# Stick-breaking attention weights: sigmoids and a running product in place of logarithms, sums and an exponential

## The chip, the core and the metric

The kernel runs on one core of a Trainium2 chip. The metric is device time in microseconds (us), lower is better. The median of three runs before the change is 1969.86 us (1965.07 to 1970.98).

The engines have short names here: PE multiplies matrices (PEld is its loading of weights), DVE is VectorE, ACT is ScalarE, POOL is GpSimd, and SP issues the transfers.

## The reference

Two blocks run one after the other on 512 tokens of 1024 features: the first has sparse attention and retention, the second a feed-forward part, a mixer, attention over a memory, and another feed-forward part. The change lies in the mixer, in its stick-breaking attention of 16 heads of 64 features. Cut to that:

```python
def stick_breaking_attention(q, k, v):
    """A[t,s] = beta_ts * prod_{s<j<t}(1-beta_tj), s<t."""
    scale = 1.0 / math.sqrt(d_)
    for i in range(s_ // SB_BLOCK):                       # blocks of 128 queries
        z = jnp.einsum('bhtd,bhsd->bhts', qb, kb) * scale  # keys up to the block's end
        causal = s_idx[None, :] < t_idx[:, None]
        log_1mb = jnp.where(causal, jax.nn.log_sigmoid(-z), 0.0)
        suffix = lax.cumsum(log_1mb, axis=3, reverse=True) - log_1mb
        log_a = jnp.where(causal, jax.nn.log_sigmoid(z) + suffix, -jnp.inf)
        outs.append(jnp.einsum('bhts,bhsd->bhtd', jnp.exp(log_a), vb))
```

A query's weight for a key is sigmoid(z) of that key times the product of sigmoid(-z) over the keys between the two.

## The kernel before

All matrix products with weights are made of three products of split numbers: the upper bits of one operand (`whi`, `a_hi`, written by ACT at L82) and the rest (`wlo`, `a_lo`, written by DVE at L83). `proj_T` (L158) gives results with the features on the partitions, `proj_X` (L203) with the tokens there. The weights come in pieces of 512 KB through three buffers `raw`.

The stick-breaking part runs over eight pairs of heads (`p`). For each pair, `proj_T` makes the queries and the keys in PSUM banks mm0 and mm1; they are split (L82, L83, L85, L86), and transfers issued by SP (L972, L975) lay them out as `Q` and `K`, two buffers each. The four query tiles of 128 then come in three groups: tiles 0 and 1 together (128 + 256 = 384 columns of scores), tile 2 (384) and tile 3 (512). A group of one head is called a unit here: 8 x 3 x 2 = 48 units. A unit goes through these steps:

- L987: the scores in one PSUM bank `sb`, two products for each query tile. Even heads use the pool `sp` (two banks), odd heads banks mm2 and mm3; the last pair uses `sp` for both.
- L991 to L993 on ACT: Abs, Exp and Ln, so that with L994 on DVE `l` becomes the softplus of the score.
- L999 on DVE: the running sum of `l` from the last key backwards. The constant `keep` holds the sum at 1e30 up to the query's own key, restarts it there and lets it run from there on. One scan for each query tile, 64 in all.
- L1000 on DVE: score minus sum, which reads the scores' bank once more; L1001 on ACT: its exponential, the weights, in one of four buffers `cs`.
- L1006 on PE: transposes into the one PSUM bank `tp`; L1008 copies them to SBUF as `aT`, on ACT for the even head and on DVE for the odd one.
- L1015 on PE: products with the values, summed in the bank `ob`; L1017 copies it out at the end of the pair, and L1022 and L1023 add up squares for the norm that follows.

That norm (L1029 to L1038) takes a logarithm and an exponential on ACT (L1034, L1035). It scales the attention's output, which is split into `oat_hi` and `oat_lo`, the second half of the features that the out-projection (L203) takes in; the first half is the state space part, transposed at L230.

The order of the instructions on each engine isn't that of the program text. A planner lays out all engines' queues when the program is built, by its own estimate of durations, and earlier text has precedence. So the next pair's projections (L158) lie between the current pair's steps on PE, and behind the last pair come the transposes L230 and the out-projection. On the chip each queue runs in the order that the plan gave it.

Of the kernel before, what the change touches and what calls it, by code (L numbers as in the profile page):

```python
# [7 lines left out]
F32 = mybir.dt.float32  # L8
F32R = mybir.dt.float32r
AF = mybir.ActivationFunctionType  # L10
ALU = mybir.AluOpType
AX = mybir.AxisListType
PSUM = bass.MemoryType.PSUM
# [9 lines left out]
# column offsets in the constant arrays  # L23
# [8 lines left out]
def block_kernel(ctx, tc, A, out, upto=99):  # L32
# [28 lines left out]
    def bcast(src, n, tile_):  # L61
        """A vector of n values on every partition."""
        nc.sync.dma_start(tile_, bass.AP(tensor=src.tensor, offset=src.offset, ap=[[0, 128], [1, n]]))
        return tile_
# [6 lines left out]
    def rpow(v, mul, eps, n=1):  # L71
        """(v * mul + eps) ** -0.5 of a [128, n] tile."""
# [6 lines left out]
    def split(hi, lo, src, scale=None):  # L79
        """hi + lo = src (times scale): the upper bits and the rest."""  # L80
# [23 lines left out]
    clock, pend = [0.0], []  # L104

    def tick(n):
        """Counts a product of n columns, and puts in what is due."""
# [13 lines left out]
    def bank(of=(0, 1, 2, 3)):  # L121
        """The next of some PSUM banks for products."""
# [6 lines left out]
    def act_get(pair, k0=0):  # L129
        """Tokens t0..t1 of feature tile k, of activations kept as [128, token tile, k, 128]."""  # L130
# [6 lines left out]
    def proj_T(src, c0, ncols, get, consume, K=8, nt=NT, splits=None, of=(0, 1, 2, 3)):  # L137
        """Features on partitions: for each 128 columns, consume(tile index, [128, tokens] in PSUM)."""
# [25 lines left out]
    def lead_T(groups, get, slots, splits=((0, 2), (2, 4))):  # L164
        """A phase's first two groups of 256 columns (source, column, consume), over the first tokens before the others."""
# [22 lines left out]
    def proj_X(src, c0, w, get, consume, K=8, nt=NT, tail=1, kp=2, korder=None, between=None, slots=()):  # L188
        """Tokens on partitions: for each token tile, consume(t, [128, w] in PSUM)."""
# [31 lines left out]
    def transpose_split(src, n, dst_pair, t, scale=None, k0=0, of=None):  # L221
        """n 128-column tiles of a token tile [128, ., 512], transposed, to hi and lo at [:, t, k0:k0+n]."""
# [28 lines left out]
    def post_pre(src, K, get, g_post, half_scale, g_pre, fg, last=False, dst=None, korder=None, slots=(), tail=1, delay=DELAY):  # L251
        """x += norm(activations @ src) [* 0.5]; returns the next phase's normalised activations."""
# [39 lines left out]
    # =====================================================================  # L292
    # first block
    # =====================================================================
    def first_block():
# [32 lines left out]
        # --- compressed, selected and window keys, values and gates; queries times -1/8  # L328
# [8 lines left out]
        def rope(xv, nh, t):  # L337
            """xv [128, nh, >=16]: rotates its first 16 columns in place."""
# [8 lines left out]
        def doubled(xv, nh):  # L347
            """Each head's 64 columns twice, transposed: [64 | 64 again, head, token] in PSUM."""
# [51 lines left out]
        # gates: 1 / (1 + exp(-x))  # L400
# [6 lines left out]
        # --- compressed blocks: the keys' hidden layer on partitions 0 to 63, the values' on 64 to 127  # L407
# [64 lines left out]
        # --- attention, three branches: scores have the sign turned, so that the least is the greatest; outputs as [2 heads x 64, token]  # L472
# [6 lines left out]
        def attention(qi):  # L479
# [4 lines left out]
            # compressed  # L484
# [27 lines left out]
            # selected, window  # L512
# [49 lines left out]
        def ev_zn(j, bank):  # L562
            """2 silu(z) = (tanh(z / 2) + 1) z"""
# [9 lines left out]
        # --- retention  # L573
# [81 lines left out]
        # --- gates of the two branches, in features layout: 2 sigmoid(m) = tanh(m / 2) + 1  # L655
# [10 lines left out]
        # --- outputs of the branches, merged  # L666
# [30 lines left out]
    # =====================================================================  # L697
    # gated feed-forward
    # =====================================================================
# [38 lines left out]
    # =====================================================================  # L738
# [486 lines left out]
```

## Time and profile before

| | |
|---|---|
| median of three runs | 1969.86 us |
| lowest and highest run | 1965.07 and 1970.98 us |
| span of the profiled execution, first to last instruction | 1963.4 us |
| busy in the span: PE, PEld, DVE, ACT | 1917.5, 1557.6, 1027.1, 773.2 us |
| the stick-breaking loop, scores of the first pair to the sum of squares of the last | 1160 to 1343 us |

The profiled execution's own time around its span isn't given; the runs above are other executions. Times in the rows below are counted from the span's start. A row of a group gives how many instructions there are, their busy time together, the mean of one in ns, and the engine's idle time just before them with what ended it. A PE instruction's end is modelled, so two that follow each other overlap as they are drawn: the time from one start to the next says what one costs. A wait put down to "issue" is one for which the profile shows no releaser. PEclk is the clock that PE was granted, as a share of 2.4 GHz.

### The profile page before, as it was taken

The page shows a single profiled execution, that of the slowest core. Times are in us where ns is not written, and L with a number is a line of the kernel's source. Part 1 is how long each engine was busy: PE and PEld are TensorE (multiplying, and loading weights), DVE is VectorE, ACT ScalarE, POOL GpSimd, SP SyncE. Part 2 cuts the span into 40 slices and gives each one's busy share as a digit, 9 for nine tenths or more (in the row PEclk, how much of TensorE's full clock was granted, in tenths as well). Part 3 has the DMA queues.
Part 4 walks back from the last instruction along what each step waited for, and adds up shares of the span by engine and source line. Part 5 has one row for each costly group of instructions (what it writes and reads, how often), then busy time and mean ns, then how long its engine had stood idle before and what let it go on. Part 6 is the DMA issues. An engine that isn't in the chain of part 4 may idle for free.

```text
span 1963.4 us, 24345 instructions
## 1 busy us (share of the span) xinstructions
PE 1917.5 (98%) x9676; PEld 1557.6 (79%) x9676; DVE 1027.1 (52%) x1751; ACT 773.2 (39%) x1332; POOL 39.2 (2%) x66
## 2 busy tenths in 40 slices
PE   7999999999999999999999999999999999999998
PEld 6777788788878888888877777667788888888887
DVE  5578743824563333323668658887464553333223
ACT  4345533223343232223545457775353432323221
POOL 0000000100000000000000000000000000000000
PEclk9999999999999999999999999999999999999999
DMA  7411033232332333324231355542262322333322
GB/s 243 129 44 33 23 97 97 83 100 86 97 101 93 97 96 97 97 97 129 83 87 43 86 135 129 129 118 68 84 192 87 97 65 86 97 97 97 97 97 86
DMA packets 153706, 191.38 MB, mean 97 GB/s; under 512 B 9748, under 2 KB 111480, under 8 KB 153464
## 3 DMA queue, kind: packets, MB, share of 16 engines
q1 hardware_dynamic: 153592, 189.82, 32.4%
q8 instruction: 76, 1.25, 0.3%
q14 instruction: 38, 0.31, 0.0%
HBM read 175.11 MB, written 2.10 MB: 90 GB/s over the span
## 4 chain that ended last, share of the span: by engine, by line
PE 84%; DVE 7%; ACT 2%; POOL 1%; issue 1%; DMA 1%; SPq 0%; POOLq 0%; DVEq 0%; ACTq 0%
PE mm L158 41%; PE mm L203 28%; PE mm L181 3%; PE ob L1015 1%; PE ob L555 1%; POOL rp_r L76 1%; DVE x_sb L273 1%; DVE cs L999 1%; PE tp L1006 1%; DVE h L245 1%; PE ob L896 1%; PE s L530 1%; PE s L1100 1%; DVE fg L266 1%; PE mm L547 1%
## 5 line engine op out<-in xcount | busy, mean ns | idle before, releaser
L83 DVE TENSOR_TENSOR wlo<-raw,whi 128x1024 fp32r<-128x1024 f32 (+1 forms) x276 | 335.8, 1217 | 652.4 <-ACT whi L82 647.1
L82 ACT ACTIVATE whi<-raw 128x1024 fp32r<-128x1024 f32 (+1 forms) x276 | 291.0, 1055 | 665.4 <-PE mm L203 282.1
L158 PE MATMUL mm<-a_hi,wlo 128*128 128x512 f32 x1120 | 439.9, 393 | 2.0 <-DVE wlo L83 1.9
L158 PE MATMUL mm<-a_hi,whi 128*128 128x512 f32 x1120 | 440.7, 393 | 0.0
L158 PE MATMUL mm<-a_lo,whi 128*128 128x512 f32 x1120 | 440.3, 393 | 0.0
L158 PEld LDWEIGHTS mm<-a_hi,wlo 128*128 128x128 f32 x1120 | 210.4, 188 | 45.5 <-DVE wlo L83 2.7
L158 PEld LDWEIGHTS mm<-a_hi,whi 128*128 128x128 f32 x1120 | 210.4, 188 | 43.5 <-issue 1.4
L158 PEld LDWEIGHTS mm<-a_lo,whi 128*128 128x128 f32 x1120 | 210.5, 188 | 43.2 <-issue 2.6
L203 PE MATMUL mm<-whi,a_hi 128*128 128x512 f32 (+1 forms) x400 | 157.2, 393 | 0.8 <-ACT whi L82 0.8
L203 PE MATMUL mm<-whi,a_lo 128*128 128x512 f32 (+1 forms) x400 | 157.2, 393 | 0.0
L203 PE MATMUL mm<-wlo,a_hi 128*128 128x512 f32 (+1 forms) x400 | 155.6, 391 | 0.0
L203 PE MATMUL mm<-whi,hid_hi 128*128 128x512 f32 x288 | 112.0, 389 | 0.0
L203 PE MATMUL mm<-whi,hid_lo 128*128 128x512 f32 x288 | 112.0, 389 | 0.0
L203 PE MATMUL mm<-wlo,hid_hi 128*128 128x512 f32 x288 | 112.0, 389 | 0.0
L203 PEld LDWEIGHTS mm<-whi,a_hi 128*128 128x128 f32 x400 | 75.7, 189 | 18.1 <-issue 2.5
L203 PEld LDWEIGHTS mm<-whi,a_lo 128*128 128x128 f32 x400 | 75.8, 189 | 15.9 <-issue 2.5
L203 PEld LDWEIGHTS mm<-wlo,a_hi 128*128 128x128 f32 x400 | 75.1, 188 | 15.0 <-issue 1.9
L76 POOL TENSOR_TENSOR rp_r<-rp_a,half 128x1 f32<-128x1 f32 (+1 forms) x58 | 37.1, 640 | 1894.0 <-DVE rp_a L74 1568.5
L203 PEld LDWEIGHTS mm<-whi,hid_hi 128*128 128x128 f32 x288 | 54.1, 188 | 11.2
L203 PEld LDWEIGHTS mm<-whi,hid_lo 128*128 128x128 f32 x288 | 54.1, 188 | 11.2
L203 PEld LDWEIGHTS mm<-wlo,hid_hi 128*128 128x128 f32 x288 | 54.1, 188 | 11.2
L82 ACT ACTIVATE hid_hi<-sg 128x512 fp32r<-128x512 f32 x44 | 27.4, 623 | 61.9 <-DVE sg L720 61.9
(442 smaller groups left out, 2961.4 us busy)
## 6 DMA issues: line engine op xcount, KB each, us to landing
raw<-in_w_in_dram SPq DMA_DIRECT2D x96, 512.0 KB, 3.7
raw<-in_ffn_w_gu_dram SPq DMA_DIRECT2D x88, 512.0 KB, 3.6
raw<-in_ffn_w_down_dram SPq DMA_DIRECT2D x44, 512.0 KB, 3.7
raw<-in_w_out_dram SPq DMA_DIRECT2D x24, 512.0 KB, 3.7
raw<-in_xa_wkv_dram SPq DMA_DIRECT2D x16, 512.0 KB, 3.7
raw<-in_w_ret_o_dram SPq DMA_DIRECT2D x8, 512.0 KB, 3.4
K<-kh SPq DMA_DIRECT2D x32, 128.0 KB, 2.4
K<-kl SPq DMA_DIRECT2D x32, 128.0 KB, 2.3
```

What stands on the lines that cost most here:

```text
L76: POOL.tensor_tensor(r[:, :n], a[:, :n], half[:, :n], op=ALU.pow)
L82: ACT.activation(hi, src, AF.Copy)
L83: V.tensor_tensor(lo, src, hi.bitcast(F32), op=ALU.subtract)
L158: PE.matmul(o, a, b, start=(kc + k == 0 and n == 0 and si == 0), stop=(kc + k == K - 1 and n == 2), skip_group_check=True)
L181: PE.matmul(banks[g][j][:, t0 * 128:t1 * 128], a, b, start=(kc + k + n + si == 0), stop=(kc == 1 and k == 3 and n == 2), skip_group_check= ...
L203: PE.matmul(banks[t][:, :w], a, b, start=(kk == 0 and n == 0), stop=(kk == K - 1 and n == 2))
L245: V.scalar_tensor_tensor(h, src, r, g, op0=ALU.mult, op1=ALU.mult)
L266: V.tensor_tensor(fgt, bank, gpost[:, hf * 512:(hf + 1) * 512], op=ALU.mult)
L273: V.scalar_tensor_tensor(xs, fg[:, t if q == 0 else NT + t % 2], r, xs, op0=ALU.mult, op1=ALU.add)
L530: PE.matmul(sbs[e], qS[:, h, qsl], kk[:, br, g, :W], start=(n == 0 and (e == 0 or nk > 2)), stop=(n == 1), skip_group_check=True)
L547: PE.transpose(tp[:, o + j], p[:, e, j * 128:(j + 1) * 128], ident)
L555: PE.matmul(ob[64 * e:64 * e + 64, a], vv[:, j, br, g * 64:(g + 1) * 64], pT[:, e, j], start=False, stop=(br == 1 and j == nk - 1), skip_g ...
```

## The change

The logarithms go. The mask is added to the scores on PE: `far` holds the identity and a triangle of -2^99 at and above the diagonal of a query tile's own 128 keys, and one more product per query tile adds it to the bank. ACT then makes sigmoid(-z) (`l`, two buffers) and sigmoid(z) (`be`, three buffers). DVE's scan forms the running product of `l` from the last key backwards, as multiply and then maximum with `own1`, whose triangle holds the product at one down to the query's own key; it lies in tiles `E2` and `E1`, which are one column longer for each query tile. `be` times that product, shifted by one key, is the weight, in one instruction per unit, or two for the first group. The table of sigmoids is preloaded in place of that of exponential and logarithm, and `keep` isn't loaded any more. The rest of the diff is comments that are left out.

```diff
-        tc.keep_in_program_order(ACT.preload_act_table_set("natural_log_exp_and_others"))
-        keep = a1.tile([128, 512], F32, name="keep")
-        nc.sync.dma_start(keep, A["c_k"])
+        tc.keep_in_program_order(ACT.preload_act_table_set("sigmoid_and_others"))
+        own1 = a1.tile([128, 512], F32, name="own1")
+        V.memset(own1[:, 0:384], 0.0)
+        V.tensor_copy(own1[:, 384:512], tri)
+        E2 = [a1.tile([128, 386], F32, name=f"E2{e}") for e in range(2)]
+        E1 = [a1.tile([128, 513], F32, name=f"E1{n}") for n in range(3)]
+        for e in E2:
+            V.memset(e[:, 128:129], 1.0)
+            V.memset(e[:, 385:386], 1.0)
+        for e in E1:
+            V.memset(e[:, 512:513], 1.0)
+        n1 = [0]
+        far = a1.tile([128, 2, 128], F32R, name="far")
+        ACT.copy(far[:, 0], ident)
+        ACT.activation(far[:, 1], tri, AF.Copy, scale=-(2.0 ** 99))
...
                             first = False
-                    l = a2.tile([128, 512], F32, name="l", bufs=4)
-                    ACT.activation(l[:, :T], sb[:, :T], AF.Abs)
-                    ACT.activation(l[:, :T], l[:, :T], AF.Exp, scale=-1.0)
-                    ACT.activation(l[:, :T], l[:, :T], AF.Ln, bias=1.0)
-                    V.scalar_tensor_tensor(l[:, :T], sb[:, :T], 0.0, l[:, :T], op0=ALU.max, op1=ALU.add)
-                    cs = a2.tile([128, 512], F32, name="cs", bufs=4)
-                    for i, off in segs:
-                        W = (i + 1) * 128
-                        rev = slice(off + W - 1, (off - 1) if off else None, -1)
-                        V.tensor_tensor_scan(cs[:, rev], keep[:, 511:(511 - W) if W < 512 else None:-1], l[:, rev], 1e30, op0=ALU.mult, op1=ALU.add)
-                    V.tensor_tensor(cs[:, :T], sb[:, :T], cs[:, :T], op=ALU.subtract)
-                    ACT.activation(cs[:, :T], cs[:, :T], AF.Exp)
-                    css.append(cs)
+                        PE.matmul(sb[:, off + i * 128:off + W], far[:, 0], far[:, 1], start=False, stop=True, skip_group_check=True)
+                    l = a2.tile([128, 512], F32, name="l")
+                    ACT.activation(l[:, :T], sb[:, :T], AF.Sigmoid, scale=-1.0)
+                    be = a2.tile([128, 512], F32, name="be", bufs=3)
+                    ACT.activation(be[:, :T], sb[:, :T], AF.Sigmoid)
+                    if len(segs) == 2:
+                        E, at = E2[e], ((0, 0), (128, 129))
+                    else:
+                        E, at = E1[n1[0] % 3], ((0, 512 - T),)
+                        n1[0] += 1
+                    for off, o in at:
+                        W = 128 if len(segs) == 2 and off == 0 else T - off
+                        rev = slice(o + W - 1, (o - 1) if o else None, -1)
+                        V.tensor_tensor_scan(E[:, rev], l[:, off + W - 1:(off - 1) if off else None:-1],
+                                             own1[:, 511:(511 - W) if W < 512 else None:-1], 1.0, op0=ALU.mult, op1=ALU.max)
+                        V.tensor_tensor(be[:, off:off + W], be[:, off:off + W], E[:, o + 1:o + 1 + W], op=ALU.mult)
+                    css.append([be[:, j * 128:(j + 1) * 128] for j in range(T // 128)])
...
-                        PE.transpose(tp[:, j], css[e][:, j * 128:(j + 1) * 128], ident)
+                        PE.transpose(tp[:, j], css[e][j], ident)
```

## Rows read from the trace of the kernel before

**Rows 1.** The page's first part: busy us, share of the span and instructions

```profile
PE 1917.5 (98%) x9676; PEld 1557.6 (79%) x9676; DVE 1027.1 (52%) x1751; ACT 773.2 (39%) x1332; POOL 39.2 (2%) x66
```

**Rows 2.** Stretches: length, busy PE, PEld, DVE, ACT, POOL; PEclk; DMA share; GB/s

```profile
1140.00:1160.00 20.00, 18.08 (x80) 14.53 (x79) 9.87 (x15) 8.03 (x14) 2.03 (x3) 1.00 0.49 127
1160.00:1343.00 183.00, 175.11 (x990) 127.82 (x989) 154.33 (x241) 135.61 (x267) 1.94 (x2) 0.98 0.49 120
1160.00:1230.00 70.00, 69.34 (x394) 51.19 (x393) 58.13 (x91) 53.05 (x107) 0.00 (x0) 1.00 0.58 136
1287.00:1314.30 27.30, 22.91 (x123) 16.12 (x122) 23.68 (x37) 19.02 (x37) 1.39 (x1) 0.87 0.64 162
1307.46:1314.29 6.83, 6.40 (x30) 4.68 (x31) 5.78 (x9) 3.33 (x6) 0.00 (x0) 0.50 0.49 104
1314.30:1343.00 28.70, 28.67 (x176) 21.62 (x175) 23.37 (x36) 20.36 (x38) 0.00 (x0) 1.00 0.17 47
```

**Rows 3.** Groups by line, 1160:1343: busy us, mean ns; idle before, its releaser

```profile
L991 ACT ACTIVATE l<-s 128x384 f32<-128x384 f32 (+1 forms) x27 | 14.2, 525 | 8.0 <-PE s L987 7.8
L991 ACT ACTIVATE l<-mm 128x384 f32<-128x384 f32 (+1 forms) x21 | 10.9, 518 | 0.2 <-PE mm L987 0.2
L992 ACT ACTIVATE l<-l 128x384 f32<-128x384 f32 (+1 forms) x48 | 25.6, 563 | 0.3
L993 ACT ACTIVATE l<-l 128x384 f32<-128x384 f32 (+1 forms) x48 | 25.7, 558 | 0.3
L1001 ACT ACTIVATE cs<-cs 128x384 f32<-128x384 f32 (+1 forms) x48 | 26.6, 558 | 9.1 <-DVE cs L1000 8.6
L1022 ACT ACTIVATE q<-ob 128x512 f32<-128x512 f32 x7 | 4.1, 590 | 2.7 <-DVE oaF L1017 2.7
L994 DVE SCALAR_TENSOR_TENSOR l<-s,l 128x384 f32<-128x384 f32 (+1 forms) x27 | 15.9, 590 | 4.9 <-ACT l L993 4.9
L994 DVE SCALAR_TENSOR_TENSOR l<-mm,l 128x384 f32<-128x384 f32 (+1 forms) x21 | 12.3, 586 | 0.0
L999 DVE TENSOR_TENSOR_SCAN cs<-keep,l 128x128 f32<-128x128 f32 (+2 forms) x64 | 50.0, 809 | 0.3
L1000 DVE TENSOR_TENSOR cs<-s,cs 128x384 f32<-128x384 f32 (+1 forms) x27 | 16.0, 592 | 0.2
L1000 DVE TENSOR_TENSOR cs<-mm,cs 128x384 f32<-128x384 f32 (+1 forms) x21 | 12.3, 587 | 0.1
L74 DVE TENSOR_SCALAR rp_a<-ss 128x1 f32<-128x1 f32 x2 | 0.3, 141 | 0.0
```

**Rows 4.** Waits in 1160:1343, PE and weight loads: total us, times, longest

```profile
PE s L987 <- DVE cs L1000: 1.9, 4, 0.6
PE tp L1006 <- ACT cs L1001: 1.7, 1, 1.7
PEld s L987 <- issue: 4.2, 8, 1.0
```

**Rows 5.** The chain's dense run, a group of the page, weight loads of the timeline

```profile
602.83 217.63 PE mm L158 x960
L158 PE MATMUL mm<-a_hi,wlo 128*128 128x512 f32 x1120 | 439.9, 393 | 2.0 <-DVE wlo L83 1.9
1224.80 0.65 PEld L987 LDWEIGHTS s<-K,Q 128*128 128x128 f32 x4
1225.38 0.19 PEld L158 LDWEIGHTS mm<-a_lo,whi 128*128 128x128 f32 x1
1225.55 0.65 PEld L987 LDWEIGHTS mm<-K,Q 128*128 128x128 f32 x4
1317.20 0.90 PEld L230 LDWEIGHTS mm<-cst,zs 128*128 128x128 f32 x8
```

**Rows 6.** The loop's table load (ns min/median/max); a later weight load

```profile
L954 ACT ACT_TABLE_LOAD  x1: 1283/1283/1283, 1146.4 to 1146.4; - x1
1353.11 0.19 PEld L203 LDWEIGHTS mm<-whi,oat_lo 128*128 128x128 f32 x1 [0.25 <-DVE oat_lo L83]
```

## The prediction

> **What bounds the kernel now.** First the page's shares: TensorE (PE) is busy 98% of the span, the next engine 52% [rows 1]. So a change pays only where PE does not stream, and work taken from another engine is worth nothing by itself. All that changes lies in the stick-breaking loop of `mixer`, so the second view is a table of stretches around it. The loop runs from 1160 to 1343 us, 183.0 us for eight pairs of heads. PE is busy 175.1 there, VectorE (DVE) 154.3, ScalarE (ACT) 135.6 [rows 2]. So DVE is at 84%, close behind PE, and a lag of DVE soon stops PE, whose queue is in order. The same table says where it does: 0.66 us of idle PE in the first 70, but 4.39 in the 27.3 us from 1287. In that stretch the granted clock stands at 0.50, the lower of its two levels (1.2 GHz), for 6.83 us, right after PE stood still most [rows 2].
>
> The third view is the groups by line: per unit (one head, one group of query tiles; 48 units) Abs 0.525 us, Exp 0.563, Ln 0.558, max-and-add 0.59, scans 1.04 (64 in 50.0 us over 48 units), subtraction 0.59, Exp 0.558 [rows 3]. (Means of two widths, 384 and 512 columns.) In series that is 4.4 us from score to weight, and the scores' PSUM bank is held through the subtraction, 3.9 us. The fourth view, who waited for whom, names it: PE's scores (L987) wait for DVE's subtraction (L1000), which lets go of a bank; transposes (L1006) wait for the last Exp (L1001) [rows 4].
>
> How much is there to win? PE's idle time is 183.0 - 175.1 = 7.9 us. That is a lower bound: a dense run has 960 products in 217.63 us, 0.227 each, while one is drawn 0.39 long [rows 5], so up to 0.17 us of each stop is hidden under the drawn end. The weight loads' waits show it: ahead of the even heads' scores they total 4.2 us where PE's own row says 1.9 [rows 4]. Twice 7.9 is 15.8, the upper bound; I take 12, about the middle.
>
> **The change part by part.** *ACT.* Four activations a unit become two, Sigmoid of z and of -z, both straight from PSUM like Abs. The trace has no Sigmoid; the nearest row is Abs (0.525 and 0.518), and the highest of the four is 0.563. Taken as Abs: out go 14.2 + 10.9 + 25.6 + 25.7 + 26.6 = 103.0 us, in come 2 x 25.1 = 50.2, so ACT's 135.6 become 82.8 [rows 2, 3]. Not on the path by itself.
>
> *DVE.* The max-and-add goes (15.9 + 12.3 = 28.2). The subtraction (16.0 + 12.3 = 28.3) becomes a product of two SBUF tiles; in the first group it is two products, of 128 and 256 columns. The columns are the same; the 16 further instructions cost at least what a DVE instruction of one column takes, 0.141 us [rows 3]: 28.3 + 2.3 = 30.6 us. The scan has the same sizes and reversed views with other operations (multiply, then max); I take it unchanged, as the nearest row is the scan itself. At the subtraction's price it would be 21.7 us less, at twice its own 50.0 more, which would make DVE the bound; both are far, and neither is in my range. DVE: 154.3 - 56.5 + 30.6 = 128.4, 70%. Small settings at the start (seven one-column memsets, own1) fall in a stretch where DVE is busy 9.87 of 20 us [rows 2] and cost nothing; without that cover under 2 us.
>
> *Latency and banks.* Score to weight becomes Abs-like 0.525, scan 1.04, product 0.64 (30.6 / 48) = 2.2 us instead of 4.4, since the second Sigmoid runs beside the scan. The bank goes free after two activations, 1.05 us instead of 3.9, so the wait of L987 for L1000 should vanish.
>
> *PE.* New is the matmul with `far`, one for each query tile of each head: 4 x 2 x 8 = 64 of 128 columns. This lies wholly on the path. By columns alone it is 128/512 of 0.227, 0.057 us: 3.6 us in all. From above: four score products of 768 columns and one wide product take 1225.55 - 1224.80 = 0.75 us; less 0.227 and less 512 columns at 0.227, two 128-column ones are left with 0.296, 0.148 each: 9.5 us. Between them eight transposes of 128 columns in a row load every (0.90 - 0.14) / 7 = 0.109 us, weights bound [rows 5]. I take that, because `far` follows a wider product under which its load begins: 7.0 us.
>
> A page of the Trainium skill gives another price: "TensorE: Matmul & The Clock Gate", section "Back-to-back issue gap", has sustained pairs of load and matmul of 128 columns at some 81 ns, an estimate of 5.2 us for the 64 and a total 1.8 better than mine; the row here is 0.109, and the sum goes by the row.
>
> *Buffers.* `l` goes from four buffers to two, the weights from four to three. A second Sigmoid can then wait for the transposes three units back; behind it on ACT are the copy L1008 of the even head and the weights' upper parts (L82), and PE waits for both. Price: nothing to the 1.7 us that PE now waits for ACT's L1001; I take nothing, because a unit holds its buffers half as long as before. The load of `keep` on SP's queue goes: nobody waited for it.
>
> *Tables.* The preload is one for one. But the logarithm of the norm behind the loop (L1034) now needs a table that is no longer there: one more load of 1.283 us [rows 6] between loop and out-projection. Cover: the state space half of that projection, PE's filler during the last pair (28.67 busy of 28.70 us [rows 2]). There is no slack otherwise: the first load of the attention half waits 0.25 us for `oat_lo` now [rows 6]. The last pair should finish sooner and leave more filler; I take nothing, and 1.3 us if the cover is gone.
>
> **The sum.** The waits: 12 us, of which the rate of the calm stretch stays, 0.66/70 of 183 = 1.7; gone 10.3. The low clock took half of the 6.40 us that PE was busy in it, 3.2 [rows 2]; with the standstill before it gone, it goes. So -10.3 - 3.2 + 7.0 = -6.5 us. The span was 1963.4; the median of the runs is 1969.86, so some 6.5 us lie around it, unchanged. Forecast: 1969.86 - 6.5 = 1963.4 us. With the bounds, 6.2 gone (7.9 - 1.7), clock unchanged and 9.5 added is +3.3; 15.8 gone with the clock and 3.6 added is -15.4.
>
> **The rivals.** (a) *A wash*: the waits shrink only by the drawn 6.2 us and the low clock stays; with 7.0 to 9.5 added, +0.8 to +3.3: 1971 to 1973. For it: the gain and the new PE work are of one size. (b) *Slower*: the waits move instead of going. Place: one PSUM bank for transposes (`tp`), so each head's transposes wait for the other's copy L1008, and the products for both; these waits are 48 a loop whatever comes before. If the plan, with shorter chains, puts them earlier in PE's queue, PE stops as long as before and `far` comes on top: +7.0 to +9.5, 1977 to 1979. It decides when under 1.1 us of waits go at 7.0, under 3.6 at 9.5. Against: in the first 70 us the same copies stop PE for under 1%. (c) *The logarithm's table lands on the path*: -6.5 + 1.3 = -5.2, 1964.7. The Trainium skill, "ScalarE: Activation LUTs", section "What ACT_TABLE_LOAD costs", puts every switch of sets at some 2.66 us with the drain, and its advice to stay in one set speaks against this change; by that the total would be -3.8. The trace agrees on the load itself, 1283 ns. (d) *More*: the starved stretch at 1287 fills completely, 15.8 gone: -15.8 - 3.2 + 7.0 = -12, 1958. (e) *The change does not do it*: were Copy or Square not usable beside Sigmoid, a unit would pay two loads, 48 x 2 x 1.283 = 123 us on ACT, 206 in all, over PE's 183: +23 or more, 1993. Against: Square (L1022) runs in this loop now, among Exp and Ln, with the one load of L954 [rows 3, 6].
>
> **How the numbers follow.** Some 0.3% (5.9 us) is what a measurement here can tell from nothing. Chances: forecast 0.50 (1958 to 1967; two thirds of it beyond 5.9 us), (a) 0.13, (b) 0.16, (c) 0.09, (d) 0.10, (e) 0.02. Faster 0.33 + 0.10 = 0.43; same 0.17 + 0.13 + 0.09 = 0.39; slower 0.18. Leaving out (b) and (e) and the far ends of the rest, the range is 1957 to 1974.
>
> **What would show it.** ACT near 83 us and DVE near 128 in the loop; no PE wait for a DVE product at L987; 64 `far` loads some 0.11 us apart from what follows; clock 1.00 throughout; a 1.28 us table load at the logarithm with PE busy through it. Wrong would be: `far` costing well over 0.15 us each; a new PE wait for copies as long as the old ones; or the idle PE after 1287 staying with DVE unloaded, which would mean that PE's filler had run out there, not that DVE was late.

## The result, and the profile after

The changed kernel takes 1986.49 us (median; 1984.61 to 1987.15), the kernel before 1968.96 beside it: 1.0091 of its time, 95% interval 1.0079 to 1.0104. It is 17.5 us slower, where 6.5 us faster was forecast. Its span is 1984.6 us, of before 1963.4. A kernel's time below is the median of its runs without two that fell in a slower state, 2382.92 us of `a_farpv` and 5189.52 us of the kernel before.

What was forecast of ACT and DVE came. The page's first part of the changed kernel, as [rows 1]; then its groups by line in 1162 to 1347 us, where its loop lies (columns as in [rows 3]):

```profile
PE 1928.7 (97%) x9740; PEld 1568.1 (79%) x9740; DVE 1006.7 (51%) x1728; ACT 731.8 (37%) x1240; POOL 38.4 (2%) x66
```

```profile
L1006 ACT ACTIVATE l<-s 128x384 f32<-128x384 f32 (+1 forms) x27 | 14.3, 529 | 13.1 <-PE s L1004 10.8 <-DVE E L1017 2.1
L1008 ACT ACTIVATE be<-s 128x384 f32<-128x384 f32 (+1 forms) x27 | 14.3, 528 | 0.3 <-PE tp L1024 0.3
...
L1017 DVE TENSOR_TENSOR_SCAN E<-l,own 128x128 f32<-128x128 f32 (+2 forms) x64 | 50.0, 812 | 4.9 <-ACT l L1006 4.5
L1019 DVE TENSOR_TENSOR be<-be,E 128x128 f32<-128x128 f32 (+2 forms) x64 | 28.8, 480 | 1.0
```

A Sigmoid costs what Abs did, the scan what it did, the product 28.8 us where 30.6 was worked out [rows 3]. Next the stretches of the changed kernel (columns as in [rows 2]): the first holds the same PE work in every table of this kind below, from the first projection product of the attention part to the 200th product of the output projection.

```profile
1143.46:1398.33 254.87, 234.62 (x1275) 176.67 (x1273) 165.80 (x265) 116.21 (x211) 2.59 (x4) 0.98 0.42 108
1162.00:1347.00 185.00, 171.27 (x1009) 126.25 (x1008) 129.19 (x206) 87.86 (x168) 1.49 (x2) 0.99 0.46 114
1189.50:1192.90 3.40, 3.33 (x12) 2.63 (x12) 3.12 (x7) 2.56 (x6) 0.00 (x0) 0.53 0.88 224
1367.00:1373.83 6.83, 5.80 (x14) 4.54 (x15) 2.72 (x3) 0.00 (x0) 0.00 (x0) 0.51 0.53 151
```

DVE stands at 129.2 us and ACT at 87.9 in the loop, against 154.3 and 135.6 [rows 2], and PE is idle 13.7 us of it, against 7.9. So PE stops more, beside engines that have less to do. Who it waits for, 1155 to 1400 us of the changed kernel (total us, times, longest):

```profile
PE tp L1024 <- DVE be L1019: 8.2, 10, 1.5
PE mm L203 <- DVE wlo L83: 4.6, 1, 4.6
PE ob L1033 <- DVE aT L1026: 1.7, 8, 0.3
...
PEld tp L1024 <- issue: 9.3, 27, 1.7
```

The scores' waits for a bank [rows 4] are gone but for one of 0.3 us, as forecast. In their place the transposes wait for DVE's product, and a product of the output projection waits 4.6 us for its weights' lower part. PE's weight loads of the changed kernel around one of its two longest stops of the first kind (the other is at 1283):

```profile
1187.27 0.19 PEld L1004 LDWEIGHTS mm<-far 128*128 128x128 f32 x1
1187.39 0.30 PEld L1001 LDWEIGHTS mm<-K,Q 128*128 128x128 f32 x2
1187.68 0.19 PEld L1004 LDWEIGHTS mm<-far 128*128 128x128 f32 x1
1189.54 0.14 PEld L1024 LDWEIGHTS tp<-cst,be 128*128 128x128 f32 x1 [1.67 <-issue]
1189.57 0.26 PEld L1001 LDWEIGHTS s<-K,Q 128*128 128x128 f32 x1
```

And DVE at that time, in its timeline:

```profile
1186.50 1.23 DVE L83 TENSOR_TENSOR wlo<-raw,whi 128x1024 fp32r<-128x1024 f32 x1 [3.80 <-ACT whi L82]
1187.64 0.68 DVE L86 SCALAR_TENSOR_TENSOR ql<-mm,qh 128x512 fp32r<-128x512 f32 x1
1188.25 0.99 DVE L1017 TENSOR_TENSOR_SCAN E<-l,own 128x128 f32<-128x128 f32 x2
1189.16 0.60 DVE L1019 TENSOR_TENSOR be<-be,E 128x128 f32<-128x128 f32 x2
```

The queue has scores and mask products of several chains in one burst, and directly behind them the first transposes of the pair. At 1187.68 all scores before them are loaded; DVE has just split weights and queries of a later pair, makes the first chain's scan and product, and the transposes load 1.86 us later. Right after that the granted clock is at its lower level (1.2 GHz) for 3.4 us. The projection products that could stand between run in bulk at other places, 34 in a row from 1203.5 to 1211.1, for one. In the kernel before the transposes lie further behind their scores, with projection products between. Its weight loads at about the same place:

```profile
1187.78 0.19 PEld L158 LDWEIGHTS mm<-a_hi,wlo 128*128 128x128 f32 x1
1188.01 0.19 PEld L158 LDWEIGHTS mm<-a_hi,whi 128*128 128x128 f32 x1
1188.24 0.48 PEld L1006 LDWEIGHTS tp<-cst,cs 128*128 128x128 f32 x3
```

The timelines give a measure of this: the work that PE has, its idle time taken off, from the start of a pair's first activation on scores (Abs, or Sigmoid of -z) to the start of its first transpose. In the kernel before it is 5.5 us (mean of the eight pairs, 4.5 to 6.3), and PE waits at none of these transposes. In the changed kernel it is 1.1 us (0.9 to 1.6), while the chain takes 1.8 us even where nothing holds it up; so PE is idle there in every pair, 7.7 us in all.

After the loop the second wait, in DVE's and PE's timelines of the changed kernel:

```profile
1354.58 0.69 DVE L1054 TENSOR_TENSOR rstd<-rstd 128x512 f32<-128x512 f32 x1 [1.25 <-ACT rstd L1053]
...
1366.76 1.22 DVE L83 TENSOR_TENSOR wlo<-raw,whi 128x1024 fp32r<-128x1024 f32 x1
```

```profile
1363.06 0.39 PE L203 MATMUL mm<-whi,a_lo 128*128 128x512 f32 x1
1368.03 0.79 PE L203 MATMUL mm<-wlo,a_hi 128*128 128x512 f32 x1 [4.59 <-DVE wlo L83]
```

Between these two DVE instructions lie the norm's last steps, the eight scalings of the outputs and seven of their eight splits; the weights' lower part comes behind them, PE stands, and then has 6.83 us of the low clock.

### The profile page after: what moved, and what is told of

The parts are those of the page before. It is cut to its first block, busy times and chain, and to the rows that moved or that the text cites. A ratio compares the mean times of both kernels' runs of the same rounds, so it can differ in the third digit from the quotient of the medians.

```text
span 1984.6 us, 24423 instructions
## 1 busy us (share of the span) xinstructions
PE 1928.7 (97%) x9740; PEld 1568.1 (79%) x9740; DVE 1006.7 (51%) x1728; ACT 731.8 (37%) x1240; POOL 38.4 (2%) x66
## 4 chain that ended last, share of the span: by engine, by line
PE 82%; DVE 9%; ACT 2%; issue 1%; POOL 1%; DMA 1%; SPq 0%; POOLq 0%; DVEq 0%; ACTq 0%
PE mm L158 41%; PE mm L203 27%; PE mm L181 3%; DVE E L1017 2%; PE ob L555 1%; POOL rp_r L76 1%; DVE x_sb L273 1%; PE ob L1033 1%; DVE h L245 1%; DVE be L1019 1%; PE ob L896 1%; PE s L530 1%; PE s L1118 1%; PE mm L547 1%; DVE fg L266 1%
## 5 line engine op out<-in xcount | busy, mean ns | idle before, releaser
L1017 DVE TENSOR_TENSOR_SCAN E<-l,own 128x128 f32<-128x128 f32 (+2 forms) x64 | 50.0, 812 | 4.9 <-ACT l L1006 4.5
```

Of the source, the lines that this page charges most:

```text
L1017: V.tensor_tensor_scan(E[:, rev], l[:, off + W - 1:(off - 1) if off else None:-1], own1[:, 511:(511 - W) if W < 512 else None:-1], 1.0, op ...
```

## The experiments

Each was timed beside the kernel before in the same session; "d" is its median less that one. The changed kernel has d = +17.5 us. First the parts, one at a time.

**The mask products and the tables.** `a_nofar` leaves the mask products out (and with them the mask); `b_far` puts 64 that add zeros into the kernel before; `a_table` loads the table with Ln and Exp once; `b_tables` makes the kernel before load tables behind its loop.

```diff
a_nofar, against after:
-                        PE.matmul(sb[:, off + i * 128:off + W], far[:, 0], far[:, 1], ...)
b_far, against before (far[:, 1] all zeros):
+                        PE.matmul(sb[:, off + i * 128:off + W], far[:, 0], far[:, 1], ...)
a_table, against after, ahead of osT (b_tables: "sigmoid_and_others", against before):
+        tc.keep_in_program_order(ACT.preload_act_table_set("natural_log_exp_and_others"))
```

> The changed kernel without the 64 products that add the mask on PE (the mask is left out, so the weights of later keys are not taken out). Theory of the prediction: these products cost 64 times 0.109 to 0.148 us, so the time falls by 7 to 9.5 us. Rival (they hide in waits that PE has anyway in the loop): it falls by under 3 us. Rival (they also stretch the order of the queue): by over 10 us.

> The kernel before with the same 64 products added to the scores, adding zeros. If each costs what the changed kernel's weight loads show, 7 to 9.5 us more than before, 1976 to 1978. If the plan of before hides them in its waits, under 3 us more. If over 10, a product more in the scores disturbs PE's order.

> The changed kernel, with the table of exponential and logarithm loaded right behind the loop's last activation, so that the norm's logarithm and exponential find it there and no table load lies between them. Theory 1 (the norm's chain is on the path: in the changed kernel two loads of 1.28 us stand in it, PE then waits 5.0 us for one wlo and runs 6.83 us at the lower clock): the chain comes 2.6 us sooner, the wait of 5.0 falls to 2.4 or less, the low clock behind it goes: 3 to 8 us less than the changed kernel, 1978 to 1983. Rival (the loop itself has lost the time, the end only shows it): within 1.5 us of the changed kernel.

> The kernel before with the table of sigmoids loaded behind the loop, so that the norm pays the table loads that the changed kernel pays, and nothing else is changed. Theory 1: the norm's chain was without slack before (the first load of the attention half waited 0.25 us), so two loads of 1.28 us in it cost 2 to 8 us (the wait itself, and the lower clock if it follows). Rival (the filler covers it): under 1 us.

| kernel | us | d | ratio, interval |
|---|---|---|---|
| a_nofar | 1969.16 | +1.5 | 1.0010 (1.0000 to 1.0019) |
| b_far | 1974.92 | +7.3 | 1.0037 (1.0023 to 1.0051) |
| a_table | 1984.75 | +17.1 | 1.0090 (1.0074 to 1.0106) |
| b_tables | 1970.42 | +2.8 | 1.0017 (1.0007 to 1.0026) |

The 64 products cost 7.3 us in the kernel before (by the interval 4.5 to 10.0; 7.0 was forecast), and 17.5 - 1.5 = 16.0 in the changed one. The rest of the change is worth about nothing: half the chain's length gone, and +1.5 us where the prediction without its mask products would have -13.5. The tables are not it: with one load in place of two, d falls by 0.4, less than the intervals, and three loads in the norm of the kernel before cost 2.8 us.

The stretch of the same work in `a_nofar`, and its waits, as for the changed kernel above:

```profile
1142.59:1380.04 237.45, 226.81 (x1210) 167.29 (x1209) 164.01 (x265) 116.13 (x209) 2.59 (x4) 0.99 0.44 116
```

```profile
PE tp L1020 <- DVE be L1015: 3.0, 7, 0.8
...
PE mm L203 <- DVE wlo L83: 1.3, 1, 1.3
```

254.87 - 237.45 = 17.4 us, 7.8 of it busy PE (mask products, and more of the low clock) and 9.6 idle. Of the idle time 8.2 - 3.0 = 5.2 us are waits of transposes for the product and 4.6 - 1.3 = 3.3 the stop at the output projection. In `b_far` no transposes wait for a product; there the scores wait for the bank more than before [rows 4]. This wait, and the stretch of the same work:

```profile
PE s L990 <- DVE cs L1004: 6.6, 8, 1.2
```

```profile
1145.01:1388.12 243.11, 230.34 (x1275) 171.97 (x1274) 189.51 (x288) 157.55 (x305) 3.42 (x4) 1.00 0.44 113
```

So the 7.3 us are not the products' own time alone: PE is idle 243.11 - 230.34 = 12.8 us here, against 9.8 in the kernel before (its stretch stands further below), and the 6.83 us of the low clock that the kernel before has in this part [rows 2] are missing (clock 1.00).

**Place or amount.** Does it matter where the 64 stand? `a_far1st` has them first in their bank; `a_farpv` (no mask) adds 64 of zeros to the output bank, where no sigmoid waits for them.

```diff
a_far1st, against after, ahead of the two score products of a query tile instead of behind them:
+                        PE.matmul(sb[:, off + i * 128:off + W], far[:, 0], far[:, 1], start=first, ...)
-                        PE.matmul(sb[:, off + i * 128:off + W], far[:, 0], far[:, 1], start=False, ...)
a_farpv, against after without the mask products, behind the value products, for both heads (far[:, 1] all zeros):
+                    for i, off in segs:
+                        PE.matmul(ob[:, i * 128:(i + 1) * 128], far[:, 0], far[:, 1], start=False, ...)
```

> The changed kernel with the mask product as the first of its score bank instead of the last: same products, same count. Known by now: the changed kernel takes 1986.5 us, without the mask products 1969.2, and 64 such products put into the kernel before cost 7.0 us. Theory 'place' (the 10 us beyond the 7 come from the mask product standing between the last score and the two sigmoids, so that it lengthens each chain and the plan lays the work around it differently): 1975 to 1980 us. Theory 'amount' (they come from 7 us more TensorE work in the attention part, wherever it stands): 1984 to 1988 us.

> The changed kernel without its mask (that part of the computation is left out), but with 64 products of the same shape and type, of zeros, added to the output bank behind the value products, where no sigmoid waits for them. Theory 'place': 1969 + 7 = 1976 us, 1974 to 1979. Theory 'amount': 1984 to 1988 us.

`a_far1st`: 1987.26 us, d = +20.5 (interval of the ratio 1.0083 to 1.0117). `a_farpv`: 1980.89, d = +14.1, that is 12.6 over `a_nofar`. The place in the bank gains nothing; off the chain they cost a little less but still well over the 7.3 of `b_far`, between the two theories.

**Without mask products, all computed.** The weight is also the difference of neighbouring running products, E[k+1] - E[k], zero by itself where the scan is held at one. That needs neither the mask products nor sigmoid(z). `a_diff` is this; `a_difffar` adds 64 products of zeros to it.

```diff
a_diff, against after (mask products and sigmoid(z) out):
-  V.tensor_tensor(be[:, off:off + W], be[:, off:off + W], E[:, o + 1:o + 1 + W], op=ALU.mult)
+  V.tensor_tensor(be[:, off:off + W], E[:, o + 1:o + 1 + W], E[:, o:o + W], op=ALU.subtract)
```

> The whole computation in another form: one sigmoid(-z), the running product E of it, and the weights as differences of neighbouring products E[k+1] - E[k], which are zero at masked keys by themselves: neither mask products nor sigmoid(z). ScalarE about 17 us less in the loop than in the changed kernel (32 x 0.53 us). If the loop is set by TensorE's own work and its order: as the changed kernel without mask products, 1967 to 1970 us. If shorter chains alone bunch the attention work (the rival): 1972 to 1977 us, slower than that kernel.

> The form with differences (1964.5 us, one sigmoid a chain, no mask products) with 64 products of the mask's shape put back last in the score banks, adding zeros. Theory 'amount' (64 products more in the attention part bring, besides their 7 us, as much again in waits of TensorE in this order): 1978 to 1983 us. Theory 'chain' (the waits come from mask product and two sigmoids in one chain together): 1971 to 1974 us.

`a_diff`: 1964.52 us, d = -2.3, ratio 0.9990 (0.9980 to 0.9999). `a_difffar`: 1985.24, d = +18.1. So 20.4 us for 64 products in chains with one sigmoid, above what either theory gave: that of mask product and two sigmoids together falls. The waits of `a_difffar`, as above:

```profile
PE tp L1023 <- DVE be L1018: 8.5, 9, 1.4
PE mm L203 <- DVE wlo L83: 4.3, 1, 4.3
```

In `a_diff` the same two are 1.1 and 1.7 us. The 64 products bring the same two waits as in the changed kernel. But it isn't they that bring the transposes forward. `a_diff` has no mask products, and its first transposes of a pair stand behind scores too; its weight loads:

```profile
1210.25 0.36 PEld L998 LDWEIGHTS mm<-K,Q 128*128 128x128 f32 x2
1210.54 0.19 PEld L158 LDWEIGHTS mm<-a_hi,whi 128*128 128x128 f32 x1
...
1211.10 0.53 PEld L998 LDWEIGHTS mm<-K,Q 128*128 128x128 f32 x3
1212.21 0.14 PEld L1019 LDWEIGHTS tp<-cst,be 128*128 128x128 f32 x1 [0.59 <-DVE be L1014]
```

By the measure given above (work of PE from a pair's first sigmoid to its first transpose) `a_nofar` has 1.8 us and `a_diff` 1.5, the changed kernel 1.1 and `a_difffar` 0.9; `b_far`, with the long chain and the 64 products, has 4.9. The step from 5.5 to under 2 comes with the shorter chains. With the 64 products there is less still: mask products fill places where `a_nofar` and `a_diff` have longer scores and projection products. The idle PE at these eight places is 7.7 us in the changed kernel and 8.3 in `a_difffar`, against 2.5 and 1.9.

**Buffers, text order, tail.** `a_be4` gives the weights four buffers. `a_pipe` writes the next pair's projections between the units of this one, with the table of `a_table`. `a_slot` gives the fourth weight group of the output projection a buffer of its own, with that table; `a_diffs` is the form with differences with both and four weight buffers.

```diff
a_be4, against after:
-                    be = a2.tile([128, 512], F32, name="be", bufs=3)
+                    be = a2.tile([128, 512], F32, name="be", bufs=4)
a_pipe, behind each unit's chain (some(n): the next n groups of 3 products):
+                    some(2)
a_slot, for group 3 of the output projection's first half:
-            hl = wload(src, ko[ch * kp], min(kp, K - ch * kp), c0, w)
+            hl = wload(src, ko[ch * kp], min(kp, K - ch * kp), c0, w, pre.get(ch))
```

> The changed kernel with 4 buffers for the weights (be) instead of 3, as many as the kernel before had. Theory 'buffers' (sigmoid(z) of a fourth chain can't start before the transposes of the first have read their weights, so the queue takes these transposes early, right behind a burst of scores, and TensorE stands at them): the waits of the transposes for DVE's product fall from 8.2 to under 5 us, 1980 to 1983 us. Rival (buffers were rightly taken at nothing): 1985 to 1988 us, waits 7 to 9 us.

> The changed kernel, the table with both Ln and Exp loaded once behind the loop, and the 48 projection products of the next pair written in groups of three or six between the units of this pair, instead of all ahead of the pair. Theory 'few fillers' (in the changed kernel the projections run in bulk and the transposes then wait for DVE's product, 8.2 us in ten waits, with work of the tail pushed late): 1973 to 1979 us. Theory 'own work and tail' (what the loop loses is the mask products' own time, the rest arises after the loop): 1983 to 1986 us.

> The changed kernel, the table with Ln and Exp loaded once, and a buffer of its own for the fourth group of the output projection's weights, so that their split needn't wait for the second group's products. Theory 'tail' (TensorE stands 4.6 us at that group because its low parts come behind the norm chain on DVE, and the low clock follows from that stop): the stop under 1 us, 1977 to 1981 us. Rival (the stop only moves to the first product that needs the norm's result): 1983 to 1985 us, as with the table alone (1984.75 us).

> The form with differences, 4 buffers for the weights, the table with Ln and Exp loaded once, and the own buffer for the fourth group of the output projection's weights: whole computation. Theory 'tail': 1.7 us of stop at that group and 1 to 2 us of loads and low clock go: 1960 to 1963 us. Rival (they move elsewhere): 1964 to 1966 us.

`a_be4`: 1986.92 us (d +19.8), the transposes wait 8.2 us as in the changed kernel: not the buffers of the weights. `a_pipe`: 1982.67 (+15.9), between the theories, and no test of either: the queue still has the projections largely in bulk, and the transposes wait 7.0 us. The order of the text is not that of the queue. `a_slot`: 1983.74 (+16.6); the stop stays at 2.9 us, so the buffer was not what held the weights back in it. The two halves of that group, in its timelines of ACT and DVE:

```profile
1356.12 1.07 ACT L82 ACTIVATE wx<-raw 128x1024 fp32r<-128x1024 f32 x1
1369.52 1.21 DVE L83 TENSOR_TENSOR wx<-raw,wx 128x1024 fp32r<-128x1024 f32 x1
```

The upper half is done at 1357.2, and DVE makes the lower one 12 us later without having waited: it stands in DVE's queue behind the eight scalings and splits of the norm's output. `a_diffs`: 1962.64 (-4.5; 0.9976, 0.9967 to 0.9984), without that stop: 1.9 us better than `a_diff`, d against d 2.2, with three things changed at once and intervals that overlap.

**The order by hand.** Left among the causes considered is the order in which PE's queue is laid out. `a_hand` pins each PE instruction of the loop behind the one before it in the text, and the text has groups of three or six projection products, those of later pairs, between scores, transposes and value products; with the table of `a_table` and four weight buffers, which alone gave nothing. `a_diffhand` is the form with differences in it.

```diff
+            scores(G0, 0, c0); some(1); scores(G0, 1, c0); some(2)
+            scores(G1, 0, c1); some(1); scores(G1, 1, c1); some(1)
+            turn(G0, 0, c0, t0); some(1); turn(G0, 1, c0, t0); some(1); values(G0, t0)
+            scores(G2, 0, c2); scores(G2, 1, c2); some(2)
+            turn(G1, 0, c1, t1); some(1); turn(G1, 1, c1, t1); some(1); values(G1, t1); some(2)
+            turn(G2, 0, c2, t2); some(1); turn(G2, 1, c2, t2); some(2); values(G2, t2)
```

> The changed kernel (mask products, two sigmoids, all as it was; 4 weight buffers, which alone changed nothing, and the table with Ln and Exp loaded once) with TensorE's order in the loop written out by hand: the projection products of the following pairs in groups of three or six between scores, transposes and value products, so that each transpose stands at least nine such products behind its scores. Theory 'order' (what the mask products cost beyond their own 7 us is the order that the plan lays out with them): the waits of the transposes for DVE's product, 8.2 us in ten, fall under 2 us, and the time to before + 7 or less: 1966 to 1976 us. Rival (64 products in this part cost 17 us in any order): 1980 to 1986 us.

> The form with differences (whole computation, no mask products, one sigmoid) in the same order by hand. Theory 'order': 7 us less than the changed kernel in that order, 1956 to 1964 us. Rival (its own plan has only 1.1 us of such waits, so there is little to gain, and the hand order lacks work for the last pair): 1964 to 1970 us.

1983.78 us (d +16.1), on the rival's side, and 1979.91 (+12.2), above what either theory gave. But the wait is another one; of `a_hand`, its largest, and DVE and weight loads at one of them:

```profile
PE ob L1054 <- DVE aT L1046: 13.9, 15, 2.5
```

```profile
1219.12 1.80 DVE L1035 TENSOR_TENSOR_SCAN E<-l,own 128x384 f32<-128x384 f32 x2
1220.84 1.00 DVE L1037 TENSOR_TENSOR be<-be,E 128x384 f32<-128x384 f32 x2
1221.76 0.55 DVE L1046 COPY aT<-tp 128x384 f32<-128x384 f32 x1
...
1222.36 0.62 PEld L1054 LDWEIGHTS ob<-aT,vv 128*64 128x64 f32 x6 [1.71 <-DVE aT L1046]
```

No transposes wait for the product any more, but the odd head's copy comes on DVE behind scans and products of later chains, and the value products behind it stand. `a_hand2` and `a_diffhand2` put both copies on ACT, and six products instead of three ahead of the value products.

```diff
-            (V.tensor_copy if e else ACT.copy)(aT[:, :T // 128], tp[:, :T // 128])
+            ACT.copy(aT[:, :T // 128], tp[:, :T // 128])
```

> The order by hand of a_hand, with both copies of the transposes on ScalarE instead of one on VectorE, six projection products instead of three between the second transposes and the value products, and the first pairs' projections 6 products further ahead. In a_hand the waits for DVE's product were gone as expected, but TensorE stood 13.9 us in 15 waits of the value products for the copy on VectorE, which comes there behind the scans of later chains. Theory 'order': these waits fall under 4 us, the time to 1968 to 1975 us. Rival (no order of this queue is much better than the plan's, since each stop only moves to the next product): 1980 to 1985 us again.

> The form with differences in the order of a_hand2. In a_hand and a_diffhand the mask products cost 1983.8 - 1979.9 = 3.9 us, part of them beside waits. Theory 'own time': with the waits gone they cost their 7 us, so 1961 to 1968 us, 6 to 8 us under a_hand2. Rival 'order makes them dear in any case': 10 to 17 us under a_hand2.

`a_hand2`: 1966.23 us, d = -1.0, ratio 0.9994 (0.9984 to 1.0004). `a_diffhand2`: 1956.25, d = -11.0, ratio 0.9943 (0.9928 to 0.9957). `a_hand2` computes all that the changed kernel does, and is 18.5 us better, d against d. Its stretch of the same work and its largest waits:

```profile
1146.78:1377.62 230.84, 220.81 (x1272) 170.77 (x1273) 148.15 (x236) 125.20 (x229) 2.20 (x4) 0.99 0.46 119
```

```profile
PE tp L1044 <- ACT aT L1046: 3.4, 3, 2.3
PE mm L203 <- DVE wlo L83: 3.4, 1, 3.4
```

Idle PE is 10.0 us there, against 20.3 (and 3.0 in a stop of its own just ahead of the stretch). The stop at the output projection is still 3.4; the waits of transposes for the product are gone: PE has 4.5 us of work between first sigmoid and first transpose.

The waits are only half of the gain. Another part lies in the value products. Their groups in the changed kernel (1143 to 1399 us) and in `a_hand2` (1146 to 1378):

```profile
L1033 PE MATMUL ob<-aT,vv 128*64 128x128 f32 (+1 forms) x288 | 34.7, 297 | 2.2 <-DVE aT L1026 1.7
L1054 PE MATMUL ob<-aT,vv 128*64 128x128 f32 (+1 forms) x288 | 25.1, 294 | 0.5 <-ACT aT L1046 0.5
```

The same 288 instructions take 9.6 us less. In the planned order the even head's first product runs by itself, ahead of the odd head's transposes, and the odd head's last one too; in the order by hand all products of both heads follow in one row, one of each head starting within 0.01 us of the other. The kernel before (35.6 us) and `a_diff` (34.7) lack this as well, and `a_diffhand2` (25.3) has it, so it is a gain of its own and no part of what the change lost.

Between `a_hand2` and `a_diffhand2` lie 10.0 us, for mask products and second sigmoid together, against 20.4 from `a_diff` to `a_difffar` in the planned order. The stretch of `a_diffhand2`:

```profile
1146.98:1368.12 221.14, 214.35 (x1209) 163.72 (x1210) 146.74 (x236) 105.27 (x181) 2.20 (x4) 0.99 0.47 124
```

220.81 - 214.35 = 6.5 us are busy PE, at the same mean clock: the products' own time. 3.2 more are idle.

**Two controls.** `a_actcopy` moves the copies alone, in the plan's order, with the table of `a_table`; `b_hand2` is the kernel before in the order of `a_hand2`, copies on ACT.

```diff
a_actcopy, against after with the table of a_table:
-                    (V.tensor_copy if e else ACT.copy)(aT[:, :T // 128], tp[:, :T // 128])
+                    ACT.copy(aT[:, :T // 128], tp[:, :T // 128])
```

> A control for a_hand2: the changed kernel with the table with Ln and Exp loaded once and both copies of the transposes on ScalarE, in the plan's own order. Theory 'order' (a_hand2's 20 us are the order's): 1981 to 1987 us, the transposes' waits for DVE's product still 7 us or more. Rival 'copies' (the copies moved off VectorE bring the gain): 1966 to 1976 us.

> The kernel before (sums of logarithms, no mask products) with the order of a_hand2 and both copies on ScalarE. Theory 'order alone': the order is worth to it what it was to the form with differences (1964.5 to 1956.3 us, 8 us), 1957 to 1962 us, so the change stays dearer than the kernel before by its mask products in this order too. Rival 'chain': between the last score of a chain and its first transposes stand some 9 to 12 projection products and scores, 3 to 4 us; the chain of the kernel before takes 4.4 us from score to weight, so TensorE waits in each pair, and ScalarE, with 135 us in the loop and the copies on top, comes late: 1966 to 1980 us, and the change pays in this order.

`a_actcopy`: 1984.86 us (d +17.2), the transposes wait 7.2 us: the copies alone give nothing. `b_hand2`: 1988.60 (+20.9; 1.0103, 1.0087 to 1.0120), on the side of 'chain' and above its range. Its stretch of the same work, and its waits:

```profile
1147.75:1401.52 253.77, 220.47 (x1209) 165.04 (x1209) 173.80 (x259) 170.44 (x324) 2.57 (x4) 0.97 0.43 108
```

```profile
PE tp L1026 <- ACT cs L1019: 15.4, 12, 2.9
PE tp L1026 <- ACT aT L1028: 13.6, 14, 1.8
```

The chain of 4.4 us doesn't fit between scores and transposes of this order: they wait for the last Exp, and for copies on an ACT that is busy 170 us of 254. In this order the changed kernel is 21.9 us better than the one before, d against d; in the plan's it is 17.5 worse.

## Why the prediction was wrong

The forecast was -10.3 (waits) - 3.2 (low clock) + 7.0 (mask products); 17.5 + 6.5 = 24.0 us separate it from the result. `a_nofar` divides them: without the mask products -13.5 would have been forecast and +1.5 was measured, 15.0 us; the mask products cost 16.0 in place of 7.0, the other 9.0.

- **ACT, DVE, latency, banks**: right. 87.9 and 129.2 us where 82.8 and 128.4 were worked out, and one wait of scores for a bank, 0.3 us.
- **The mask products' own cost**, 7.0 us wholly on the path: right in size, 6.5 us of busy PE from `a_diffhand2` to `a_hand2`, 0.101 each. That `b_far` gave 7.3 is partly luck: in it the own time stands beside 3.0 us more of idle PE and a low clock that is gone. The Trainium skill's 81 ns ("TensorE: Matmul & The Clock Gate", "Back-to-back issue gap") would have made 5.2, an estimate; the 0.101 is nearer to the row of 0.109. That they would cost no more than this was wrong.
- **The waits, "gone 10.3"**: this step failed. It shortened each chain in a queue taken as it was: the transposes would stand where they stood, and find their weights ready. But PE's queue was laid out anew, with the first transposes of a pair right behind a burst of scores, 1.1 us of PE's work after the first sigmoid instead of 5.5. So the waits moved: idle PE over the same work is 254.87 - 234.62 = 20.3 us, 237.45 - 226.81 = 10.6 without the mask products, and in the kernel before, whose stretch of the same work stands here, 9.8:

```profile
1141.66:1376.99 235.33, 225.52 (x1211) 167.84 (x1210) 187.00 (x288) 158.16 (x303) 3.42 (x4) 0.99 0.46 117
```

- **The low clock, "it goes"**: failed with that step. It moved to the new stops, 3.4 us after the one at 1187.7, and 6.83 after that at 1363.
- **Rival (b)** named the mechanism and its reason: shorter chains, the transposes earlier in PE's queue, the waits moving, the mask products on top. `a_nofar` and `a_diff` bear the reason out, with their transposes as early. Wrong are its place, as DVE's product L1019 is waited for and not the copies L1008, and its size, 7.0 to 9.5. In the changed kernel's plan the products cost 16.0 us: over the same work 7.8 us more of busy PE, 5.2 in the transposes' waits, 3.3 in the stop behind the loop, and 1.1 in other stops (`a_nofar` against the changed kernel).
- **Buffers at nothing**: right for the weights' (`a_be4`). That `l` has two instead of four was not tried alone. Some sigmoids do wait for a scan to let go of `l` (2.1 us in the row of L1006 above, 5.4 for odd heads), but none of the first ones of a pair, behind which the transposes wait most.
- **Tables at nothing, rival (c)**: nearly right. Two loads lie in the norm, not one: Ln and then Exp each load their own unless one table with both is loaded ahead. The stop at the output projection is 4.6 us with them and 3.0 with one load; the time moves by less than can be told. Of the 2.66 us a switch of the Trainium skill ("ScalarE: Activation LUTs", "What ACT_TABLE_LOAD costs") the traces show 1.28 for the load; three loads in the norm of the kernel before cost 2.8 us in all, part of them beside other work. The stop itself was not foreseen: its cover, PE's filler [rows 2, 6], is there, but the weights' lower part stands in DVE's queue behind the norm's results.
- **That the order is the cause** of what the mask products cost beyond their own time is shown by two pairs: 20.4 us for them in the planned order (`a_diff`, `a_difffar`), 10.0 with the second sigmoid in the order by hand. `a_hand2` does the changed kernel's work in 18.5 us less, but about half of that is the value products, which the loss has nothing to do with; the tables alone give 0.4, the buffers nothing, copies and tables 0.3. How far ahead the projections run is part of that order and was not tried alone. The orders of DVE and ACT were planned anew with it.
- **Open**: why the plan puts the transposes that early once the chains are short, and earlier still with 64 products more. Its estimates of durations are not on record.

## What to carry to other kernels

Where an order is planned from the work itself, a change costs not only its own instructions but brings a new order of everything: read PE's queue after an edit before pricing any wait as gone, and price the same addition in two orders (7.3 us in the kernel before, 16.0 in the changed one) to tell the two apart. A shorter chain is worth something only in an order that uses it: the same pair of kernels differed by +17.5 us in the planned order and by -21.9 in one written for short chains. And an operation may be saved altogether: a weight that is the difference of two neighbours of a running product needs no mask and no second sigmoid; with the order by hand it made the fastest kernel, 1956.25 us.

## What the runs showed of the hardware that was not expected

Sixty-four products of 128 columns cost 7.3, 12.6, 16.0 and 20.4 us in four surroundings, though the median step from such a load to the next is 0.11 to 0.14 us in all four (1187.27 to 1187.39 above, for one). The same 288 instructions of value products take 34.7 us in one order and 25.1 in another, in which each has one of the other head beside it. A stop of PE, 1.86 us from load to load, was followed by the lower clock level (0.53 granted for 3.4 us from 1189.5), so a stop can cost more than its length; another of the same 1.86 us, from 1282.65 in the same kernel, was not (clock 1.00 from 1284.5 to 1288). An Ln followed by an Exp loaded two tables, at 1350.19 and 1352.62 us, 1.28 us each.
